# Prompt attention: the gate is scaled by 1/sum before the products, two low-query buffers change places, and three gate writes change queues

## The chip, the cores and the metric

The kernel runs on one core of a Trainium2 chip. The metric is the device time of one execution in microseconds (us). Before the change the median of three runs is 2872.78 us (2870.52 to 2873.95).

The core has five engines with an instruction stream each: TensorE (PE, matrix products and transposes; PEld are its weight loads), VectorE (DVE), ScalarE (ACT), GpSimd (POOL) and SyncE (SP, which here only issues DMAs). An engine runs its instructions in the order of its stream, and an instruction that waits holds up all that stand behind it. PSUM is the memory that PE writes its products to.

## The reference

The kernel is one step of a two-layer decoder over a prompt of 1024 rows (with 16 meta rows ahead of it) and 64 sample rows. Layer one is an mLSTM mixer with a feed-forward block, layer two a "forgetting attention" with a gate, and a feed-forward block again. The change lies in the prompt's attention of layer two:

```python
def fox_attention(q, cq, pos_q, k, v, ck, pos_k):           # cut: one block of 128 query rows
    s = einsum('bqhd,bkhd->bhqk', qi, k)
    s = s + ci[..., None] - ckT[:, :, None, :]
    s = where(pos_k[None, :] <= pi[:, None], s, -inf)
    p = softmax(s, axis=-1)
    return einsum('bhqk,bkhd->bqhd', p, v)

def fox_mixer(xn, shared, attend, w_qo, q_g, w_out):
    ...
    og = p[..., HD:]
    o = attend(q, k, v, lf).reshape(B, T, HD)
    return (o * jax.nn.sigmoid(og)) @ w_out
```

There are 16 heads of 64 columns. The softmax is not normalised before the product with v: the kernel forms exp(s - max) v, and the division by the row's sum is folded into the gate's factor, so that each output element is (exp(s - max) v) * sigmoid(og) * 1/sum. Which of the two factors comes first does not matter to the mathematics.

## The kernel before, in words

**Where the part lies.** `attend_prompt` (L2456) runs from about 1770 to 2023 us of the profiled execution. Ahead of it stands the sample rows' attention, in which PE's gaps are filled with the gate projections `gates()` (L2089): for seven of eight blocks of 128 gate columns, PE multiplies, ACT takes the sigmoid (L2105) and POOL's queue writes it to the tensor `og2D` in device memory (L2106). Behind `attend_prompt` comes the output projection and the last feed-forward block.

**Units.** Heads are taken in pairs (`hp` 0 to 7), and the two heads of a pair are called z = 0 and 1; they lie on partitions 0 to 63 and 64 to 127 of the query and key tiles. Query rows are taken in groups of 256 (`g`, in the order QG = 0, 3, 1, 2), each of two blocks u of 128 rows. A group g has g + 1 units of up to 256 keys; the last unit of a group is its tail. That makes 32 groups, each with a tail, and 80 units.

**Score pieces.** `scores()` cuts a block's keys into pieces of up to 512 (KSPLIT). A piece takes two PSUM buffers named `sp`, one for each z, out of three. PE writes both with six matmuls (L2596: high queries by high keys, high queries by low keys, low queries by high keys). Then DVE, first for z = 0 and then for z = 1, adds the forget terms (`ncb`, or `nd` on the diagonal), keeps the row's maximum (L2600, each with a short read of the maximum into `mx`) and so frees the buffer. POOL computes the exponent's bias `nb` and the next diagonal `nd` (L2566); ACT takes the exponentials and their sums `sm` (L2623).

**A unit.** `turn` transposes the exponentials on PE into a PSUM tile `tp` (L2650, L2654; there are two such tiles, of two banks each); ACT copies it to `th` (L2658), and at a tail 16 further rows to `tail` (L2660). At a tail DVE also takes the reciprocal of the sums (L2663, `r`) and POOL spreads it over 64 columns (L2666, `rx`). `prod` multiplies `th` with the values into the PSUM tile `op` (L2683 to L2691; there is one such tile, shared by all groups, so the next group's first product waits until DVE has read it).

**The tail before the change.** `prod` first transposes `rx` on PE with four small matmuls (L2678): two go into the free part of `tp` (head 0 of the pair), two into the free part of `op` (head 1). After the products DVE computes `og = op * og` on 128x256 (L2694) and then twice `og = rs * og` on 128x128 (L2697), once with rs out of `tp`, once out of `op`. POOL then splits the result into a high and a low part.

**Order.** PE, DVE, ACT and POOL run this part in the order in which the code is written. The loop over groups and units writes, for each unit: score pieces that are due (`ahead`), the unit's `turn`, exponentials, further pieces (`ahead`), and then the `prod` of the unit before (`late`). Pieces run nine ahead (LEAD). Between the first nine pieces stand the steps of `last_gate`, the eighth block of gate columns in 24 steps of three matmuls (L266 to L268): six steps ahead of the first piece and two after each of the nine. Its three sigmoids (L2483) use the `tp` tiles.

**Query and key tiles.** `load_k` loads four tiles of a head pair: high queries, high keys, low keys and, after the forget terms, low queries (`qDl`). Even head pairs use four of the weight slots that earlier phases leave, odd ones four tiles of their own. The last slot, `slots[8]`, is the weight slot that the last gates of `gates()` read.

Of the kernel before, what the change touches and what calls it, by code (L numbers as in the profile page):

```python
# [8 lines left out]
F32R = mybir.dt.float32r  # L9
# [7 lines left out]
P = 128  # L17
# [1946 lines left out]
def phase_b(self, ys, w7, cb):  # L1964
# [121 lines left out]
    with self.pool("spp") as sp, self.pool("sp2", bufs=2) as s2, self.pool("gb", bufs=3) as fp, \  # L2086
            self.pool("spps", bufs=2, space=PSUM) as pp:
        def gates():

            for m in range(7):  # L2090
                if m == 4:

                    self.w7 = gate(7, keep=w7)
                wh, wl = gate(m) if m else w0
                for t, (t0, t1) in enumerate(TS):
                    if (m, t) == (0, 0):
                        continue
                    n = t1 - t0
                    ps = pp.tile([P, 512], F32, name=self.uid("bps"), tag="b", bufs=3)
                    xh, xl = self.X[t]  # L2100
                    for k in range(KT):
                        self.mm3(ps[:, :n], wh[:, k, :], wl[:, k, :], xh[:, k, :], xl[:, k, :], k == 0, k == KT - 1)
                        if k == KT - 1:
                            s = fp.tile([P, SL], F32, name=self.uid("ogb"), tag="ogb")
                            nc.scalar.activation(s[:, :n], ps[:, :n], AF.Sigmoid)  # L2105
                            nc.gpsimd.dma_start(self.og2D[m, :, t0:t1], s[:, :n])  # L2106
                        yield

        with self.tc.manual_schedule(engines={mybir.EngineType.PE}):
            self.attend_sample(sk, sp, s2, pp, cq, ncn, masks, ys, gates())  # L2110
# [345 lines left out]
def attend_prompt(self, ys, slots, both, w):  # L2456
# [3 lines left out]
    with self.pool("ap", bufs=1) as sp, self.pool("ap2", bufs=2) as s2, self.pool("app", bufs=2, space=PSUM) as pp:  # L2460
# [34 lines left out]
        heads = {}  # L2495

        def place_k(hp):
            if hp % 2 == 0:
                return [slots[x][:, :NP] for x in (2, 7, 3, 8)]
            return [s2.tile([P, NP], F32R, name=f"{nm}_{hp}", tag=f"{nm}1", bufs=1) for nm in ("qh", "kh", "kl", "ql")]  # L2500

        def place_c(hp):
            return s2.tile([P, 2, NP], F32, name=f"ncb_{hp}", tag="ncb1", bufs=1) if hp % 2 else both
# [31 lines left out]
        firstv = [s2.tile([P, 9, P], F32, name="vr0", tag="vr")]  # L2535
        firsto = [s2.tile([P, 256], F32, name="og0_0", tag="ogP", bufs=8)]
        first[1], firstc[1] = place_k(1), place_c(1)
        for qb in (6, 5, 7):
            firsts.update({(qb, z): row(0, qb, z) for z in range(2)})
        for qb in (3,):  # L2540
# [26 lines left out]
                                        in1=mask.unsqueeze(1).broadcast_to([P, 2, P]), op=ALU.add)  # L2567

        rows = {}

        def scores(hp, g):

# [6 lines left out]
            for u in range(2):  # L2579
# [11 lines left out]
                for n in KSPLIT[qb]:  # L2591
                    ps = [pp.tile([P, 512], F32, name=f"sp{hp}_{qb}_{c}_{z}", tag="sp", bufs=3) for z in range(2)]
                    for y, (a, b) in enumerate(((qh, kh), (qh, kl), (ql, kh))):
                        for z in range(2):
                            r = slice(z * 64, z * 64 + 64)
                            nc.tensor.matmul(ps[z][:, :n], a[r, qs], b[r, at : at + n], start=(y == 0), stop=(y == 2))  # L2596
                    parts = [(0, n)] if at + n < nk else [(0, n - P), (n - P, n)]
                    for z in range(2):
                        for y, (o, e) in enumerate(parts):
                            nc.vector.tensor_tensor_reduce(  # L2600
                                out=ss[z, u][:, at + o : at + e], in0=ps[z][:, o:e],
                                in1=diag[x][:, z] if y else ncb[:, z, at + o : at + e], scale=1.0,
                                scalar=mx[:, z, c + y - 1 : c + y] if c + y else NEG, op0=ALU.add, op1=ALU.max,
                                accum_out=mx[:, z, c + y : c + y + 1])
# [21 lines left out]
        def units(hp, g):  # L2626
# [8 lines left out]
            for j0 in range(0, nf, 2):  # L2635
# [3 lines left out]
                def turn(j0=j0, tail=tail, hold=hold):  # L2639
# [19 lines left out]
                    if tail:  # L2659
# [5 lines left out]
                            [P, 2, 2, DH], F32, name=f"rx{hp}_{g}", tag="rx")  # L2665
                        nc.gpsimd.tensor_copy(rx, hold["r"].unsqueeze(3).broadcast_to([P, 2, 2, DH]))  # L2666

                def prod(j0=j0, tail=tail, hold=hold):
                    th = hold["th"]
                    mm = nc.tensor.matmul  # L2670
                    if tail:


                        hold["rs"] = [hold["pt"][:, 0, 6:], po[:, 256:384].rearrange("p (u q) -> p u q", u=2)]
                        for u in range(2):
                            for h, x in enumerate(hold["rs"]):
                                r = slice(h * 64, h * 64 + 64)
                                mm(x[:, u], hold["rx"][r, u].rearrange("p z d -> p (z d)"), self.ident[r, r],  # L2678
                                   start=(h == 0 or j0 == 0), stop=True, is_transpose=True, skip_group_check=True)
                    ds = [slice(z * 64, z * 64 + 64) for z in range(2)]  # L2680
                    for x in range(1 if tail else 2):
                        for z in range(2):
# [9 lines left out]
                               start=False, stop=(u == 1))  # L2692
                    y = og[g]
                    nc.vector.tensor_tensor(out=y, in0=po[:, :256], in1=y, op=ALU.mult)  # L2694
                    for h, x in enumerate(hold["rs"]):
                        yh = y.rearrange("p (u h q) -> p h u q", u=2, h=2)[:, h]
                        nc.vector.tensor_tensor(out=yh, in0=x, in1=yh, op=ALU.mult)  # L2697
                    c0 = T0 + 256 * g
                    for t, (t0, t1) in enumerate(TS):
                        a, b = max(c0, t0), min(c0 + 256, t1)  # L2700
# [5 lines left out]
                            nc.gpsimd.tensor_tensor(out=xl[:, hp, xs], in0=ya, in1=xh[:, hp, xs].bitcast(F32),  # L2706
                                                    op=ALU.subtract)

                out.append((turn, prod))
            return out  # L2710

        groups = [(hp, g) for hp in range(8) for g in QG]
# [10 lines left out]
        with tc.manual_schedule(engines={E.PE, E.DVE, E.Activation, E.Pool}):  # L2723
# [4 lines left out]
                masked(x)  # L2728
            todo, gate = pieces(), last_gate()
            made = 0  # L2730
            for _ in range(6):
                next(gate, None)

            def ahead(slot):

                nonlocal made
                while made < ns and made < LEAD + slot * ns / (2 * nu):
                    next(todo, None)
                    made += 1
                    if slot == 0:  # L2740
                        for _ in range(2):
                            next(gate, None)
                        exps(len(todo_exp) - 1)

            late = None
            slot = 0
            todo_exp = []
            for hp, g in groups:
                us = None
                for k in range(g + 1):  # L2750
# [13 lines left out]
                        n = max(n - m, 0)  # L2764
                    us[k][0]()
                    exps(n)
                    ahead(slot + 1)
                    if late:
                        late()
                    late = us[k][1]  # L2770
                    slot += 2
                    if g == QG[1] and k == 2 and hp < 7:
                        load_v(hp + 1, nc.sync)
# [7 lines left out]
            late()  # L2781
    return ws


# [32 lines left out]
```

## Time and profile before

| | before |
|---|---|
| median of three runs | 2872.78 us |
| profiled execution, its own time | 2874.75 us |
| its span in the profile | 2873.1 us |
| mean granted clock of TensorE | 0.997 |
| instructions in the profile | 53648 |
| median of the runs less the profiled execution | -1.97 us |

The span is the stretch from the first to the last instruction of the profiled execution, and 1.65 us of its own time lie around it. A row of the timeline names a start and a duration in us, the engine, the line of the kernel, the operation, the output tile and its inputs, the shape and how many stand in the row; in square brackets stands the idle time of the engine just ahead of it and what ended that idle time. The view of the waits lists, for one engine, the line that waited, the instruction that released it, the sum in us, the number of times and the longest. The view by stretches gives the busy time of PE, PEld, DVE, ACT and POOL in a stretch, each with its number of instructions, and then the granted clock, the share of busy DMA engines and GB/s. The ends of PE's instructions are modelled, and neighbours overlap in the rows, so that starts are read rather than ends.

### The profile page before, as it was taken

How to read it: one execution, taken by the hardware profiler on the slowest of the kernel's cores; microseconds unless marked ns; L12 is line 12 of the kernel's file. 1: busy time of each engine (PE TensorE's matmuls, PEld its weight loads, DVE VectorE, ACT ScalarE, POOL GpSimd, SP SyncE). 2: the span in 40 equal slices, each digit the busy share in tenths (PEclk: the TensorE clock that was granted, in tenths of full speed). 3: DMA queues.
4: the chain of work that ended last, by engine and by line, in shares of the span. 5: the costliest groups of instructions: out<-in, count | busy, mean ns of one | idle time of the engine just before them, and what ended most of it. 6: DMA issues, size and time to landing. Idle time of an engine off the chain costs nothing.

```text
span 2873.1 us, 53648 instructions
## 1 busy us (share of the span) xinstructions
PE 2795.3 (97%) x20485; PEld 2674.7 (93%) x20485; DVE 1726.0 (60%) x3478; ACT 1310.9 (46%) x2622; POOL 1017.8 (35%) x1495
## 2 busy tenths in 40 slices
PE   7999989999999999999999999999999999999999
PEld 7998979999999999999999888677999999999999
DVE  6044555887777655553345444776478777765553
ACT  6122464444444434443444444777344444443432
POOL 3022333075556311115352102454307655531210
PEclk9999999999999999999999999999999999999999
DMA  7057656122222275544453676442413222237652
GB/s 214 16 144 170 164 159 182 49 88 78 79 84 78 98 264 197 203 150 136 139 174 123 238 279 220 143 148 85 158 48 94 75 75 84 78 98 255 219 184 101
DMA packets 312443, 400.19 MB, mean 139 GB/s; under 512 B 28142, under 2 KB 235050, under 8 KB 311162
## 3 DMA queue, kind: packets, MB, share of 16 engines
q1 hardware_dynamic: 277234, 277.79, 30.4%
q0 software_dynamic: 33728, 118.38, 12.6%
q8 instruction: 161, 2.64, 0.4%
q14 instruction: 96, 0.79, 0.1%
q10 hardware_dynamic: 1224, 0.60, 0.1%
HBM read 299.92 MB, written 96.77 MB: 138 GB/s over the span
## 4 chain that ended last, share of the span: by engine, by line
PE 69%; DVE 10%; issue 4%; ACT 3%; DMA 2%; POOL 1%; DVEq 0%; ACTq 0%; POOLq 0%; SPq 0%
PE m L1505 23%; PE dps L266 6%; PE dps L268 6%; PE dps L267 6%; PE tmps L266 3%; PE tmps L267 3%; PE tmps L268 3%; DVE slot L339 2%; PE sp L2596 1%; DVE s L2600 1%; PE op L2683 1%; PE pops L266 1%; PE pops L267 1%; PE pops L268 1%; PE bps L266 1%
## 5 line engine op out<-in xcount | busy, mean ns | idle before, releaser
L339 DVE TENSOR_TENSOR slot<-slot,slot 128x1024 fp32r<-128x1024 f32 (+3 forms) x263 | 266.5, 1016 | 133.9 <-ACT slot L338 125.4
L338 ACT CAST slot<-slot 128x1024 fp32r<-128x1024 f32 (+3 forms) x263 | 206.7, 788 | 236.3 <-PE dps L267 90.1
L1505 PE MATMUL m<-x1h,slot 128*128 128x384 f32 x640 | 178.3, 338 | 3.1 <-DVE ns L1481 1.5
L1505 PE MATMUL m<-x0h,slot 128*128 128x336 f32 x640 | 167.0, 316 | 0.0
L413 POOL TENSOR_TENSOR ns<-ns,nq 128x384 f32<-128x384 f32 (+1 forms) x59 | 63.8, 1081 | 210.9 <-ACT nq L411 209.7
L1505 PE MATMUL m<-x2h,slot 128*128 128x384 f32 x480 | 135.8, 337 | 0.0
L1612 POOL DMA_DIRECT2D hr<-hT x60 | 32.5, 542 | 281.6 <-DVE T_2l L339 68.8
L108 POOL TENSOR_TENSOR slot<-vA 128x256 f32<-128x256 f32 x80 | 74.9, 946 | 151.2 <-DMA vA<-in_w_gate_up 147.5
L108 POOL TENSOR_TENSOR slot<-Ht 128x256 f32<-128x256 f32 x80 | 74.9, 946 | 150.9 <-DMA Ht<-in_w_gate_up 147.2
L339 DVE TENSOR_TENSOR slot<-Ht,slot 128x256 fp32r<-128x256 f32 (+3 forms) x101 | 84.9, 842 | 63.6 <-ACT slot L338 63.6
L339 DVE TENSOR_TENSOR slot<-vA,slot 128x256 fp32r<-128x256 f32 (+3 forms) x101 | 85.5, 849 | 62.2 <-ACT slot L338 62.2
L1505 PEld LDWEIGHTS m<-x1h,slot 128*128 128x128 f32 x640 | 117.1, 188 | 4.4 <-DVE ns L1481 2.1
L1505 PEld LDWEIGHTS m<-x0h,slot 128*128 128x128 f32 x640 | 113.3, 188 | 0.0
L1505 PE MATMUL m<-x1l,slot 128*128 128x384 f32 x320 | 107.8, 337 | 0.0
L1505 PE MATMUL m<-x0l,slot 128*128 128x336 f32 x320 | 101.0, 316 | 0.0
L1505 PE MATMUL m<-T_2h,slot 128*128 128x384 f32 x320 | 96.8, 343 | 3.0 <-ACT Ht L1511 0.9
L2623 ACT ACTIVATE s<-s,nb 128x272 f32<-128x272 f32 (+7 forms) x126 | 98.9, 786 | 0.1
L2658 ACT COPY th<-tp 128x768 f32<-128x768 f32 (+1 forms) x80 | 73.4, 919 | 55.3 <-PE tp L2650 32.6
L1505 PE MATMUL m<-T_4h,slot 128*128 128x384 f32 x320 | 95.3, 338 | 0.0
L108 POOL TENSOR_TENSOR Ht<-Ht 128x512 f32<-128x512 f32 (+1 forms) x60 | 84.5, 1408 | 28.4 <-DVE wl1l L339 28.4
L108 POOL TENSOR_TENSOR vA<-vA 128x512 f32<-128x512 f32 (+1 forms) x60 | 84.4, 1408 | 27.5 <-DVE wl0l L339 27.5
L2029 DVE TENSOR_REDUCE ss<-sqb 128x4 f32<-128x256 f32 (+1 forms) x72 | 30.2, 419 | 102.8 <-ACT sqb L2028 102.0
(843 smaller groups left out, 10286.8 us busy)
## 6 DMA issues: line engine op xcount, KB each, us to landing
slot<-in_w_down SPq DMA_DIRECT2D x88, 512.0 KB, 4.4
wr<-in_w_down SPq DMA_DIRECT2D x42, 512.0 KB, 4.7
wraw<-in_w_in_a SPq DMA_DIRECT2D x40, 512.0 KB, 4.0
vA<-in_w_gate_up SPq DMA_DIRECT2D x40, 512.0 KB, 3.9
Ht<-in_w_gate_up SPq DMA_DIRECT2D x40, 512.0 KB, 4.1
hr<-hT POOLq DMA_DIRECT2D x46, 384.0 KB, 5.5
kp<-in_cache_k SPq DMA_DIRECT2D x32, 512.0 KB, 5.6
vp<-in_cache_v SPq DMA_DIRECT2D x32, 512.0 KB, 6.3
```

The source lines that it names most:

```text
L108: self.net.nc.gpsimd.tensor_tensor(out=o, in0=a, in1=b, op=op)
L266: mm(ps, sh, mh, start=first, stop=False)
L267: mm(ps, sh, ml, start=False, stop=False)
L268: mm(ps, sl, mh, start=False, stop=last)
L338: self.nc.scalar.copy(hi, src)
L339: self.nc.vector.tensor_tensor(out=lo, in0=src, in1=hi.bitcast(F32), op=ALU.subtract)
L413: (nc.vector if x >= late else nc.gpsimd).tensor_tensor(out=s, in0=s, in1=sq, op=ALU.add)
L1505: nc.tensor.matmul(u.b[b][:, :n], w[p][:, k], x[q][:, k], start=new and k == i == 0, stop=k == 1 and i == 2, skip_group_check=True)
L1612: nc.gpsimd.dma_start(hraw[j], hT[t][:, 2 * c : 2 * c + 2])
L2029: nc.vector.tensor_reduce(out=ss[:m, i, :], in_=sq[:m].rearrange("p (h d) -> p h d", d=DH), op=ALU.add, axis=AX.X)
L2623: nc.scalar.activation(ss[z, u], ss[z, u], AF.Exp, bias=nb[:, z : z + 1], accum_out=sm[:, u, z : z + 1])
L2658: nc.scalar.copy(th.rearrange("p x z (u h q) -> p h (x z u) q", h=2, q=64)[:, :, :n], pt[:, :, :n])
```

## The change

1. **The tail.** The four transposes of `rx` (now `spread`) all go into the free part of `tp`, which has room for both heads. They are written into PE's stream right after the six matmuls of the first score piece that follows the tail's `turn`. The two multiplications of the gate by 1/sum (now `scale`) are written into DVE's stream between that piece's z = 0 and z = 1 (or, where no piece follows, ahead of the products, `flush`). After the products there is one multiplication on DVE, `og = op * og`. So `op` is read by one DVE instruction and `tp` by two that come before the products' result.
2. **Low queries.** The fourth tile of even head pairs is a tile of their own and that of odd ones is `slots[8]`. The tiles of head pair 0 are set aside early, so its low queries no longer land in the slot that the last gates read.
3. **Gate steps.** Three, not six, steps of `last_gate` stand ahead of the first score piece; the three left over follow the ninth piece.
4. **Queue.** The three writes of the seventh gate block (m = 6) are issued by ACT instead of POOL.

```diff
-                            nc.gpsimd.dma_start(self.og2D[m, :, t0:t1], s[:, :n])
+                            (nc.scalar if m == 6 else nc.gpsimd).dma_start(self.og2D[m, :, t0:t1], s[:, :n])
...
         def place_k(hp):
+            own = lambda nm: s2.tile([P, NP], F32R, name=f"{nm}_{hp}", tag=f"{nm}1", bufs=1)
             if hp % 2 == 0:
-                return [slots[x][:, :NP] for x in (2, 7, 3, 8)]
-            return [s2.tile([P, NP], F32R, name=f"{nm}_{hp}", tag=f"{nm}1", bufs=1) for nm in ("qh", "kh", "kl", "ql")]
+                return [slots[x][:, :NP] for x in (2, 7, 3)] + [own("ql")]
+            return [own(nm) for nm in ("qh", "kh", "kl")] + [slots[8][:, :NP]]
...
+        first[0] = place_k(0)
...
                     parts = [(0, n)] if at + n < nk else [(0, n - P), (n - P, n)]
+                    spread, scale = between.pop() if between else (None, None)
+                    if spread:
+                        spread()
                     for z in range(2):
+                        if z and scale:
+                            scale()
                         for y, (o, e) in enumerate(parts):
...
+                def spread(j0=j0, hold=hold):
+                    hold["rs"] = [hold["pt"][:, h, 6:] for h in range(2)]
+                    for u in range(2):
+                        for h, x in enumerate(hold["rs"]):
+                            r = slice(h * 64, h * 64 + 64)
+                            nc.tensor.matmul(x[:, u], hold["rx"][r, u].rearrange("p z d -> p (z d)"), self.ident[r, r],
+                                             start=True, stop=True, is_transpose=True, skip_group_check=True)
+
+                def scale(hold=hold):
+                    for h, x in enumerate(hold["rs"]):
+                        yh = og[g].rearrange("p (u h q) -> p h u q", u=2, h=2)[:, h]
+                        nc.vector.tensor_tensor(out=yh, in0=x, in1=yh, op=ALU.mult)
+
                 def prod(j0=j0, tail=tail, hold=hold):
                     th = hold["th"]
                     mm = nc.tensor.matmul
-                    if tail:
-
-
-                        hold["rs"] = [hold["pt"][:, 0, 6:], po[:, 256:384].rearrange("p (u q) -> p u q", u=2)]
-                        for u in range(2):
-                            for h, x in enumerate(hold["rs"]):
-                                r = slice(h * 64, h * 64 + 64)
-                                mm(x[:, u], hold["rx"][r, u].rearrange("p z d -> p (z d)"), self.ident[r, r],
-                                   start=(h == 0 or j0 == 0), stop=True, is_transpose=True, skip_group_check=True)
...
                     y = og[g]
                     nc.vector.tensor_tensor(out=y, in0=po[:, :256], in1=y, op=ALU.mult)
-                    for h, x in enumerate(hold["rs"]):
-                        yh = y.rearrange("p (u h q) -> p h u q", u=2, h=2)[:, h]
-                        nc.vector.tensor_tensor(out=yh, in0=x, in1=yh, op=ALU.mult)
...
-            for _ in range(6):
+            for _ in range(3):
                 next(gate, None)
...
+            def flush():
+                for pair in between:
+                    for f in pair:
+                        f()
+                between.clear()
...
+                    if late and late[2]:
+                        between.append(late[2])
                     ahead(slot + 1)
                     if late:
-                        late()
-                    late = us[k][1]
+                        flush()
+                        late[1]()
+                    late = us[k]
```

VectorE's stream at the tail of group 3 of head pair 0. `og_3` is the gate's tile, `op_3` the products, `tp_3_6` the tail's transposes, `sp_7_0_0` and `sp_7_0_1` the first piece of query block 7 for z = 0 and 1, `sp_7_1_0` its second piece. Before:

```order
L2600 ISA s_7_0_19140,mx_7_19142<-sp_7_0_0_19143,ncb_18561 128x512
L2600 ISA mx_7_19142 128x1
L2600 ISA s_7_1_19141,mx_7_19142<-sp_7_0_1_19144,ncb_18561 128x512
L2600 ISA mx_7_19142 128x1
L2694 TENSOR_TENSOR og_3_18595<-op_3_18893,og_3_18595 128x256
L2697 TENSOR_TENSOR og_3_18595<-tp_3_6_19058,og_3_18595 128x2x64
L2697 TENSOR_TENSOR og_3_18595<-op_3_18893,og_3_18595 128x2x64
L2600 ISA s_7_0_19140,mx_7_19142<-sp_7_1_0_19170,ncb_18561,mx_7_19142 128x272
```

The same place after the change:

```order
L2608 ISA s_7_0_19141,mx_7_19143<-sp_7_0_0_19144,ncb_18560 128x512
L2608 ISA mx_7_19143 128x1
L2687 TENSOR_TENSOR og_3_18595<-tp_3_6_19058,og_3_18595 128x2x64 x2
L2608 ISA s_7_1_19142,mx_7_19143<-sp_7_0_1_19145,ncb_18560 128x512
L2608 ISA mx_7_19143 128x1
L2706 TENSOR_TENSOR og_3_18595<-op_3_18893,og_3_18595 128x256
L2608 ISA s_7_0_19141,mx_7_19143<-sp_7_1_0_19171,ncb_18560,mx_7_19143 128x272
```

Two multiplications went from behind the products' multiplication to ahead of the z = 1 half of the piece; there are as many as before.

ScalarE's stream at the start of the prompt's attention. `ogb` are the last gates of the seventh block, `th` and `og7s` the sigmoids of the eighth, `s_1` and `s_2` the first exponentials. Before:

```order
L2105 ACTIVATE ogb_18475<-bps_18398 128x384
L2105 ACTIVATE ogb_18518<-bps_18478 128x384
L2483 ACTIVATE th_18575<-og_18606 128x336
L2623 ACT_TABLE_LOAD
L2623 ACTIVATE s_1_0_18576,smf<-s_1_0_18576,nbf 128x144
L2623 ACTIVATE s_1_1_18577,smf<-s_1_1_18577,nbf 128x144
L2623 ACTIVATE s_2_0_18578,smf<-s_2_0_18578,nb_2_18662 128x272
L2623 ACTIVATE s_2_1_18579,smf<-s_2_1_18579,nb_2_18662 128x272
L2483 ACT_TABLE_LOAD
L2483 ACTIVATE og7s_18753<-og_18667 128x384
```

After:

```order
L2105 ACTIVATE ogb_18475<-bps_18398 128x384
L2106 DMA og2D<-ogb_18475 128x384
L2105 ACTIVATE ogb_18518<-bps_18478 128x384
L2106 DMA og2D<-ogb_18518 128x384
L2631 ACT_TABLE_LOAD
L2631 ACTIVATE s_1_0_18576,smf<-s_1_0_18576,nbf 128x144
L2631 ACTIVATE s_1_1_18577,smf<-s_1_1_18577,nbf 128x144
L2483 ACT_TABLE_LOAD
L2483 ACTIVATE th_18575<-og_18606 128x336
L2631 ACT_TABLE_LOAD
L2631 ACTIVATE s_2_0_18578,smf<-s_2_0_18578,nb_2_18653 128x272
L2631 ACTIVATE s_2_1_18579,smf<-s_2_1_18579,nb_2_18653 128x272
```

The first exponentials went ahead of the eighth block's first sigmoid, which costs two more table loads, and the writes of the seventh block came into this stream.

More of the change, by code (lines that the diff above doesn't have):

```diff
@@ L2569, in attend_prompt @@
         rows = {}
+        between = []
         def scores(hp, g):
@@ L2707, in prod @@
                                                     op=ALU.subtract)
-                out.append((turn, prod))
+                out.append((turn, prod, (spread, scale) if tail else None))
             return out
@@ L2780, in attend_prompt @@
                     next(tile0)
-            late()
+            for f in late[2]:
+                f()
+            late[1]()
     return ws
```

## The prediction

> **What bounds the kernel.** I read the page's first part, then the view by stretches, then the waits of TensorE inside the prompt's attention, then the timelines of the places that these name.
>
> ```profile
> span 2873.1 us, 53648 instructions
> PE 2795.3 (97%) x20485; PEld 2674.7 (93%) x20485; DVE 1726.0 (60%) x3478; ACT 1310.9 (46%) x2622; POOL 1017.8 (35%) x1495
> 1870.00:1910.00 40.00, 37.52 (x524) 27.85 (x521) 29.72 (x147) 28.81 (x59) 20.46 (x54) 1.00 0.41 138
> 2030.00:2070.00 40.00, 40.00 (x246) 39.81 (x245) 20.24 (x29) 13.22 (x20) 13.69 (x18) 1.00 0.54 180
> ```
>
> PE sets the time: 97% busy in all, 37.52 of 40 us inside the attention, 40.00 of 40 behind it. The change removes no product, so it can win only what PE idles in the attention, and what it wins there stays won, since the stretch behind is full of PE's own work. The waits there (1765 to 2030 us):
>
> ```profile
> PE sp L2596 <- DVE mx L2600: 7.2, 17, 0.9
> PE tp L2650 <- DVE og L2697: 4.0, 7, 0.6
> ...
> PE op L2683 <- PE sp L2596: 1.0, 6, 0.2
> PE sp L2596 <- DMA slot<-qDl: 0.6, 1, 0.6
> ...
> PE op L2683 <- DVE r L2663: 0.5, 1, 0.5
> ...
> PE op L2683 <- DVE og L2697: 0.4, 2, 0.2
> ```
>
> These rows hold 13.7 us, an upper end for any gain. The sum is made against the profiled execution, 2874.75 us by its own time, which is 1.97 us above the median of the runs (2872.78).
>
> **DVE at a tail.** The first rows are DVE's, the last five POOL's, ACT's and PE's, at one group-3 tail:
>
> ```profile
> 1867.78 0.69 DVE L2600 CUSTOM_DVE_ANT_0 s<-sp,ncb 128x512 f32<-128x512 f32 x1 [1.07 <-PE op L2678]
> 1868.39 0.69 DVE L2600 CUSTOM_DVE_ANT_0 s<-sp,ncb 128x512 f32<-128x512 f32 x1
> 1869.01 0.42 DVE L2694 TENSOR_TENSOR og<-op,og 128x256 f32<-128x256 f32 x1
> 1869.53 0.29 DVE L2697 TENSOR_TENSOR og<-tp,og 128x128 f32<-128x128 f32 x1
> 1869.74 0.28 DVE L2697 TENSOR_TENSOR og<-op,og 128x128 f32<-128x128 f32 x1
> 1869.94 0.49 DVE L2600 CUSTOM_DVE_ANT_0 s<-sp,ncb,mx 128x272 f32<-128x272 f32 x1
> 1865.80 0.40 POOL L2666 COPY rx<-r 128x256 f32<-128x256 f32 x1
> 1865.15 0.25 ACT L2660 COPY tail<-tp 16x128 f32<-16x128 f32 x1
> 1867.47 0.21 PE L2678 MATMUL tp<-ident,rx 64*128 64x64 f32 x1
> 1870.14 0.44 PE L2596 MATMUL sp<-kh,qh 64*128 64x384 f32 x1
> 1871.09 0.41 PE L2596 MATMUL sp<-kh,qh 64*128 64x384 f32 x1 [0.50 <-DVE mx L2600]
> ```
>
> The first 128x128 multiplication starts 0.10 us after the end of the 128x256 one (1869.53 against 1869.01 + 0.42), whose result it needs. Where an instruction needs nothing of the one ahead, it starts 0.08 us before that one's end (1868.39 against 1867.78 + 0.69; 1869.74 against 1869.53 + 0.29). After the change the 128x128 pair needs only `rx`, and the 128x256 one needs only the second of the pair, behind which a whole score reduction lies. So each tail costs DVE 0.52 - 0.34 = 0.18 us less (I count 0.17): 0.21 + 0.20 + 0.34 in place of the 0.93 from 1869.01 to 1869.94. The ends are 0, if an instruction always waits for the one ahead, and 0.18, since the same three multiplications stay.
>
> The Trainium skill, "VectorE: DVE Perf Modes", section "The DRAIN you can't avoid", says that the pipe is flushed after every DVE instruction whatever the semaphores, so that only fewer instructions help; by it this term would be 0. The trace disagrees at these rows: 0.10 us behind the end in one case, 0.08 ahead of it in the other.
>
> **What of it reaches PE.** Three places.
>
> At this one (the second half of the piece that follows, which waits for a `sp` buffer that DVE reduces behind the tail) the 0.50 wait shrinks by 0.17. It stands at the group-3 tails of pairs 0 to 6: 7 x 0.17 = 1.2 us. Ends: 0 and 7 x 0.18 = 1.3.
>
> The next two places lie behind a group-2 tail and behind the group-0 tail after it:
>
> ```profile
> 1884.94 0.56 DVE L2600 CUSTOM_DVE_ANT_0 s<-sp,ncb 128x400 f32<-128x400 f32 x1
> 1885.43 0.57 DVE L2600 CUSTOM_DVE_ANT_0 s<-sp,ncb 128x400 f32<-128x400 f32 x1
> 1884.97 0.71 PE L2650 MATMUL tp<-ident,s 64*128 64x64 f32 x16 [0.57 <-DVE og L2697]
> 1885.46 0.49 PE L2596 MATMUL sp<-kh,qh 64*128 64x256 f32 x2
> ...
> 1888.30 0.28 DVE L2697 TENSOR_TENSOR og<-op,og 128x128 f32<-128x128 f32 x1
> 1888.73 1.08 PE L2683 MATMUL op<-th,vr 128*64 128x256 f32 x8 [0.16 <-PE sp L2596]
> ```
>
> Behind group 2, the turn waits 0.57 us until the gate's multiplication has read `tp` (the 4.0 us, 7 times). That read moves ahead, so this wait goes. But the score piece right behind the turn starts at 1885.46, as soon as DVE's reduction of 1884.94 has given its buffer back (the next one starts at 1885.43), and this reduction comes only 0.17 us earlier. I take 7 x 0.17 = 1.2 us; the other 0.4 of each should reappear as a wait of L2596 for `mx`. Ends: 0 and 7 x 0.57 = 4.0, if the piece finds a buffer free. The value is near the low end, since the reduction's row and the piece's start nearly touch.
>
> Behind group 0, group 3's first product waits 0.16 us for `op` (1.0 + 0.4 us, 8 times, put down to various releasers). The tile now comes free when the 128x256 multiplication ends, 0.17 us sooner. That is the whole wait: 8 x 0.17 = 1.4 us. Ends: 0 and 1.4.
>
> **What the moved work could cost.** The pair now holds up the z = 1 reduction by 0.21 + 0.21 = 0.42 us at every tail. In the rows above, its buffer came free at 1868.39 + 0.69 = 1869.08 and would at 1869.50, while PE asks for it at 1870.14: covered by 0.64. I cost it at nothing; with the cover gone, it is 0.42 at each tail (a rival below). The moved transposes at 1867.47 need `rx`, ready at 1865.80 + 0.40 = 1866.20, and now also that the 16 rows were copied out of `tp` (1865.15 + 0.25): 1.3 and 2.1 us of room. POOL's split of the result waits for the 128x256 multiplication alone, 0.2 us sooner.
>
> **The start.** PE, ACT and POOL as the attention begins, and an ACT-issued DMA from another phase for its price:
>
> ```profile
> 1773.77 0.54 POOL L2106 DMA_DIRECT2D og2D<-ogb  x1 [4.76 <-issue]
> 1774.50 0.34 PE L2596 MATMUL sp<-slot,slot 64*128 64x144 f32 x2 [0.65 <-DMA slot<-qDl]
> 1776.06 0.45 ACT L2483 ACTIVATE th<-og 128x336 f32<-128x336 f32 x1 [4.78 <-PE og L268]
> 1783.95 1.28 ACT L2483 ACT_TABLE_LOAD   x1 [4.00 <-issue]
> 1792.84 0.49 ACT L2483 ACTIVATE og7s<-og 128x384 f32<-128x384 f32 x1
> 1794.45 0.68 PE L2650 MATMUL tp<-ident,s 64*128 64x64 f32 x14
> 1.43 0.34 ACTq L291 DMA_DIRECT2D grows<-in_norm_ffn  x1
> ```
>
> The 0.65 wait for the low queries goes, because their tile is free early and nothing else there is late: the same piece's other four matmuls did not wait. What is late next is ACT's third sigmoid of the eighth block, whose `tp` the turn at 1794.45 takes over. The second sigmoid's gate steps end later by two pieces of some 0.8 us and sooner by 0.65, so ACT's chain from 1783.95 on moves some 0.9 back, and the third ends near 1793.33 + 0.5 = 1793.8, which is when the turn is now wanted (1794.45 - 0.65). I take 0.5 of the 0.65. Ends: 0.65 and, with the chain another 0.9 late, a loss of 0.3.
>
> Two more table loads of 1.28 lie in ACT's gaps of 4.78 and 4.00: nothing. ACT issues three DMAs at 0.34 each, two of them in the 4.78 gap and the first in the sample rows' stage: nothing, for each stands right behind its own sigmoid, and what is queued behind are the table load and the first exponentials, which have no scores yet. POOL loses 3 x 0.54 and a wait ahead of the diagonals: nothing on PE's path. The SP queue keeps its number of DMAs. The eighth block's write on POOL slips behind two small bias operations: its first reader is the last head pair's gates.
>
> **The end.** The last tails have no score piece behind them:
>
> ```profile
> 2017.05 0.43 DVE L2694 TENSOR_TENSOR og<-op,og 128x256 f32<-128x256 f32 x1 [0.25 <-PE op L2691]
> 2017.71 0.28 DVE L2697 TENSOR_TENSOR og<-op,og 128x128 f32<-128x128 f32 x1
> 2018.14 1.08 PE L2683 MATMUL op<-th,vr 128*64 128x256 f32 x8 [0.50 <-DVE r L2663]
> ```
>
> `op` is free at 2017.99 before and near 2017.56 after, once the pair fits ahead with little wait: 0.4 us of the 0.50. Ends: 0 and 0.5.
>
> **Sum.** 1.2 + 1.2 + 1.4 + 0.5 + 0.4 = 4.7 us. The profiled execution goes from 2874.75 to 2870.05, the median to 2872.78 - 4.7 = 2868.1 us, 0.16% less. About 0.2% (5.7 us; 2867.0 and 2878.5) is what a measurement of this kernel tells from no change. My own range for this case is 2866.3 to 2869.6 (gains of 3.2 to 6.5): the low gain has the start at -0.3 and half of the 1.4 missing, the high one has the wait behind group 2 shrink by 0.4 instead of 0.17 and the start at its 0.65.
>
> **Rivals.** *The waits vanish whole.* If the pieces behind group 2 find their buffer, 4.0 + 1.4 + 1.2 + 0.65 + 0.5 = 7.8 us go: 2865.0. For it speaks that the 0.57 is charged to `og` alone; against it the reduction's start beside the piece's. Also POOL's bias work follows DVE's maxima, and could move with them.
>
> *DVE saves nothing at a tail* (the flush rule above). Then only the start and the end remain, 0.9 us: 2871.9, and the waits for `og` turn into waits for `mx`. The 0.10 and 0.08 of the rows speak against it.
>
> *The pair blocks a score buffer* (slower). DVE holds the z = 1 half 0.42 us longer at all 32 tails. If PE wanted that buffer more than 0.64 us sooner than at the place shown, each tail would lose it: 32 x 0.42 - 0.9 = 12.5 us, 2885.3. At places where several short pieces stand behind a tail I know the room less well, and PE that gains elsewhere asks sooner. Half of the tails give 2878.6, the point from which it is slower.
>
> *The change does nothing*: the low queries' DMA has its early tile but waits for something else, and ACT's sigmoids cost the turn what was won. It lies inside the second rival's time, and shares its chance.
>
> **Chances.** Forecast 0.50, vanishing waits 0.25, no saving 0.13, blocked buffer 0.12. Of the forecast's own range about a quarter lies below 2867.0 (0.12) and counts as faster: faster 0.25 + 0.12 = 0.37; same 0.38 + 0.13 = 0.51; slower 0.12. The range 2864.0 to 2872.5 takes in the first three cases and leaves out the fourth and the tails of the others.
>
> **What would show it.** DVE's gap of 0.10 before L2687 gone, and 0.76 for the three multiplications together; no wait of the turn (L2658) for `og`; L2599 waiting 0.3 to 0.4 for `mx` at 1885; group 3's first product without a wait; no wait for `qDl`. Wrong I would be if L2599's waits for `mx` grow beyond 7.2 + 2.8 us, or if a wait for `rx` or the third sigmoid appears on PE.

## The result, and the profile after

The changed kernel takes 2864.39 us (median of 20 runs, 2860.56 to 2871.11), the kernel before 2869.39 us (20 runs, 2865.48 to 2873.95). The ratio is 0.9985 with a 95% interval of 0.9979 to 0.9992: 4.3 us less, between 2.3 and 6.0. The forecast was 4.7 us less, a ratio of 0.9984. (The three runs known beforehand, median 2872.78, lay high among the 20; hence the ratio, not the absolute time, is compared.)

The first part of the page of the kernel after:

```profile
span 2864.7 us, 53623 instructions
PE 2798.8 (98%) x20485; PEld 2679.3 (94%) x20485; DVE 1724.8 (60%) x3478; ACT 1313.7 (46%) x2624; POOL 1014.7 (35%) x1492
```

The view of TensorE's waits in the prompt's attention (1760 to 2025 us), after:

```profile
PE sp L2599 <- DVE mx L2608: 7.6, 23, 0.9
PE tp L2681 <- POOL rxf L2674: 1.2, 1, 1.2
PE tp L2681 <- POOL rx L2674: 1.1, 1, 1.1
PE op L2695 <- ACT th L2666: 0.2, 1, 0.2
PE tp L2681 <- ACT tail L2668: 0.2, 1, 0.2
```

Gone are the turns' waits for `og`, the first products' waits for `op` (1.0 and 0.4 us before), a turn's wait of 1.1 us for `th` near the end, the end's wait for `r` and the wait for the low queries. The wait for `mx` comes 23 times instead of 17, which is the wait that was to reappear behind group 2, and two waits for POOL's copy of 1/sum are new or longer: 1.2 us at the start, 1.1 (before 0.4) at the end.

VectorE at the group-3 tail whose rows the prediction quotes, and PE behind it, after:

```profile
1863.83 0.69 DVE L2608 CUSTOM_DVE_ANT_0 s<-sp,ncb 128x512 f32<-128x512 f32 x1 [1.05 <-PE tp L2681]
...
1864.45 0.48 DVE L2687 TENSOR_TENSOR og<-tp,og 128x128 f32<-128x128 f32 x2
1864.85 0.68 DVE L2608 CUSTOM_DVE_ANT_0 s<-sp,ncb 128x512 f32<-128x512 f32 x1
...
1865.45 0.42 DVE L2706 TENSOR_TENSOR og<-op,og 128x256 f32<-128x256 f32 x1
1865.79 0.49 DVE L2608 CUSTOM_DVE_ANT_0 s<-sp,ncb,mx 128x272 f32<-128x272 f32 x1
...
1866.94 0.41 PE L2599 MATMUL sp<-kh,qh 64*128 64x384 f32 x1 [0.32 <-DVE mx L2608]
```

The pair takes 0.40 us (1864.45 to 1864.85) and the 128x256 multiplication 0.34 (1865.45 to 1865.79): 0.74 in place of 0.93. PE's wait is 0.32 in place of 0.50.

PE behind the group-2 tail, and at the first products behind the tails of groups 1 and 0, after:

```profile
1871.48 0.66 PE L2658 MATMUL tp<-ident,s 64*128 64x64 f32 x16
1872.07 1.08 PE L2695 MATMUL op<-th,vr 128*64 128x256 f32 x8
...
1879.89 0.65 PE L2658 MATMUL tp<-ident,s 64*128 64x64 f32 x16
1880.35 0.36 PE L2599 MATMUL sp<-kh,qh 64*128 64x256 f32 x1
1881.02 0.38 PE L2599 MATMUL sp<-kh,qh 64*128 64x256 f32 x1 [0.31 <-DVE mx L2608]
...
1883.93 1.08 PE L2695 MATMUL op<-th,vr 128*64 128x256 f32 x8
```

The turn behind group 2 no longer waits, and the piece behind it waits 0.31 us in its second half. The same places before, for the first product behind group 1:

```profile
1875.62 0.66 PE L2650 MATMUL tp<-ident,s 64*128 64x64 f32 x16
1876.42 1.08 PE L2683 MATMUL op<-th,vr 128*64 128x256 f32 x8
```

From turn to product it is 0.80 us before and 0.59 after, although no view put a wait there: PE's ends are modelled and covered the idle 0.21 us.

How long the attention takes is read between two starts that both kernels share, the last sample product (L2440) and the first product of the output projection (L266). Before, then after:

```profile
1768.90 1.07 PE L2440 MATMUL pom<-ptM,vmS 16*128 16x32 f32 x8
2022.53 0.43 PE L266 MATMUL pops<-x0h,slot 128*128 128x336 f32 x1
```

```profile
1766.00 1.07 PE L2440 MATMUL pom<-ptM,vmS 16*128 16x32 f32 x8
2013.38 0.42 PE L266 MATMUL pops<-x0h,slot 128*128 128x336 f32 x1
```

That is 253.63 and 247.38 us. Cut at the first score piece of each head pair (the first row of a 64x144 `sp`), the parts are:

| stretch | before | after | difference |
|---|---|---|---|
| last sample product to the scores of pair 1 | 33.50 | 35.78 | +2.28 |
| scores of pair 1 to pair 2 | 29.06 | 28.05 | -1.01 |
| pair 2 to pair 3 | 31.62 | 29.31 | -2.31 |
| pair 3 to pair 7 (four periods) | 115.54 | 112.13 | -3.41, 0.85 each |
| pair 7 to the output projection | 43.91 | 42.11 | -1.80 |
| sum | 253.63 | 247.38 | -6.25 |

So the tails win 0.85 us in every period, and the start loses. These are single executions: the 31.62 of the third row holds a stretch of low clock that the kernel after has elsewhere (below). The 2.9 us by which the two kernels differ ahead of the attention can't be put to the change: two executions of one and the same kernel (tail and places, below) get there at 1770.06 and 1766.10 us.

### The profile page after: what moved, and what is told of

Its sections match the earlier page's. It is cut to its first block, busy times and chain, and to the rows that moved or that the text cites. A ratio compares the mean times of both kernels' runs of the same rounds, so it can differ in the third digit from the quotient of the medians.

```text
span 2864.7 us, 53623 instructions
## 1 busy us (share of the span) xinstructions
PE 2798.8 (98%) x20485; PEld 2679.3 (94%) x20485; DVE 1724.8 (60%) x3478; ACT 1313.7 (46%) x2624; POOL 1014.7 (35%) x1492
## 4 chain that ended last, share of the span: by engine, by line
PE 71%; DVE 9%; issue 4%; ACT 4%; DMA 2%; POOL 1%; DVEq 0%; ACTq 0%; POOLq 0%; SPq 0%
PE m L1505 24%; PE dps L266 6%; PE dps L268 6%; PE dps L267 6%; PE tmps L266 3%; PE tmps L267 3%; PE tmps L268 3%; PE sp L2599 2%; PE op L2695 2%; DVE slot L339 1%; PE pops L266 1%; PE pops L267 1%; PE pops L268 1%; PE bps L266 1%; PE tp L2658 1%
```

## The experiments

Theory 1 is the prediction's: the tail's work on DVE is 0.18 us shorter and frees `op` and `tp` sooner. It was widened after the profile by the place behind group 1 and by the start's new wait. The table gives for each run the ratio to the kernel before in runs on the same chip, with its 95% interval, and, from one profile each, the length of the attention as above and a period: the middle one of the four from pair 3 to pair 7. (In five of the profiles one of the four is longer, by 0.33 to 0.36.)

| run | ratio | attention, us | a period |
|---|---|---|---|
| changed kernel | 0.9985 (0.9979 to 0.9992) | 247.38 | 28.03 |
| tail alone | 0.9977 (0.9968 to 0.9986) | 246.78 | 28.04 |
| start alone | 1.0013 (1.0004 to 1.0022) | 253.31 | 28.88 |
| pair behind z = 1 | 0.9993 (0.9984 to 1.0002) | 250.71 | 28.63 |
| both halves in `tp` only | 0.9988 (0.9979 to 0.9997) | 248.88 | 28.53 |
| eighth block's writes on ACT too | 0.9978 (0.9968 to 0.9988) | 247.36 | 28.03 |
| seventh block's writes on POOL | 0.9980 (0.9971 to 0.9989) | 248.64 | 28.03 |
| tail and places | 0.9970 (0.9957 to 0.9982) | 245.23 | 28.02 |
| tail and places, again | 0.9978 (0.9969 to 0.9987) | 246.69 | 28.02 |
| tail and queue | 0.9982 (0.9973 to 0.9991) | 245.30 | 28.03 |
| six gate steps | 0.9976 (0.9966 to 0.9986) | 244.22 | 28.04 |
| changed kernel, again | 0.9981 (0.9971 to 0.9990) | 247.53 | 28.02 |

**The tail alone.** The other three parts are undone:

```diff
-(nc.scalar if m == 6 else nc.gpsimd).dma_start(self.og2D[m, :, t0:t1], s[:, :n])
+nc.gpsimd.dma_start(self.og2D[m, :, t0:t1], s[:, :n])
...
-                return [slots[x][:, :NP] for x in (2, 7, 3)] + [own("ql")]
-            return [own(nm) for nm in ("qh", "kh", "kl")] + [slots[8][:, :NP]]
+                return [slots[x][:, :NP] for x in (2, 7, 3, 8)]
+            return [own(nm) for nm in ("qh", "kh", "kl", "ql")]
...
-        first[0] = place_k(0)
...
-            for _ in range(3):
+            for _ in range(6):
                 next(gate, None)
```

> Only the tail is changed (transposes of rx and the pair of multiplications early, both halves in tp); queues, low-query places and the six gate steps are as before. Theory 1 (the tail's DVE chain is 0.18 us shorter and op comes free after one multiplication): the four places of a head pair shrink as in the changed kernel, a period of 28.0 us against 28.9, that is 0.85 x 7 to 8 = 6 to 7 us less than before (ratio 0.9977), with the 0.65 us wait for the low queries still there and no wait of PE for rxf at the start. Rival (the gain needs the whole change, or comes from the start): ratio 0.9990 or more.

Ratio 0.9977, 6.6 us less (4.0 to 9.2); the period is 28.04, the wait for the low queries is there (0.51 us), and none for `rxf`. Theory 1 holds, and the whole gain is the tail's.

**The start alone.** The kernel before with the other three parts (the same diff, the other way round).

> Only the start is changed (low-query places, three gate steps, the seventh gate block's writes on ACT's queue); the tail is as before. Theory 1: the 0.65 us wait for the low queries goes, and a wait of some 1.2 us of PE for rxf comes, because POOL's 393rd DMA, which takes 2.5 us longer to start, is now the last write of the eighth gate block and stands ahead of rxf: 0.3 to 0.6 us slower than before, ratio 1.0000 to 1.0004, period 28.9. Rival (the start wins and the tail loses): 0.9980 to 0.9990, no wait for rxf.

Ratio 1.0013, 3.7 us more (1.1 to 6.3): slower, by more than the 0.3 to 0.6 expected. The wait is where it was expected, and POOL's rows of this run show its cause:

```profile
1794.56 0.57 POOL L2484 DMA_DIRECT2D og2D<-og7s  x1 [6.24 <-issue]
1795.13 0.41 POOL L2668 COPY rxf<-rf 128x256 f32<-128x256 f32 x1
```

```profile
1791.59 0.49 ACT L2483 ACTIVATE og7s<-og 128x384 f32<-128x384 f32 x1
```

The sigmoid ended at 1792.08 and the write that needs it started at 1794.56, 2.48 us later; elsewhere such a write follows its sigmoid by some 0.3 us (before: 1792.84 + 0.49 to 1793.63). `rxf` stands behind the write on POOL, and PE behind `rxf`. In the kernel before, the same delay is at 1773.77, 2.49 us behind the sigmoid of 1770.79 + 0.49. Counted along POOL's instructions, both are the 393rd DMA that POOL issues. Of the 3.7 us, the profile shows 0.54 at the first product (27.71 us after the last sample product, 27.17 before) and 1.23 at the first scores of pair 1 (34.73, 33.50 before), a part of it by the clock (below). The rest stands in no view: the attention as a whole is here 0.3 us shorter than before, whose profile holds the low clock in its 31.62.

**The pair behind z = 1.** As the changed kernel, but:

```diff
                     for z in range(2):
-                        if z and scale:
-                            scale()
                         for y, (o, e) in enumerate(parts):
...
+                    if scale:
+                        scale()
                     at += n
```

> As the changed kernel, but on DVE the pair of multiplications by 1/sum stands behind both halves of the score piece, next to the multiplication that needs its result. Theory 1 (the gain is the 0.18 us that a dependent neighbour costs): the 0.10 us gap comes back, the period goes back to 28.6 to 28.9, and the time is that of before, ratio 0.9995 to 1.0005. Rival A (it is enough that the pair comes before the products): period 28.0, ratio 0.9985. Rival B (holding up the z = 1 half costs 0.4 us a tail): faster than the changed kernel, ratio below 0.9975.

Ratio 0.9993 and a period of 28.63. DVE at a group-3 tail of this run:

```profile
1858.27 0.48 DVE L2687 TENSOR_TENSOR og<-tp,og 128x128 f32<-128x128 f32 x2
1858.86 0.42 DVE L2706 TENSOR_TENSOR og<-op,og 128x256 f32<-128x256 f32 x1
1859.20 0.49 DVE L2606 CUSTOM_DVE_ANT_0 s<-sp,ncb,mx 128x272 f32<-128x272 f32 x1
```

The 128x256 multiplication starts 0.11 us after the pair's end (1858.75), the three together take 0.93 again (1858.27 to 1859.20), and PE's wait there is back at 0.51. Both rivals fall: it is not enough that the pair comes ahead, and holding up the z = 1 half costs less than the gap does. Behind group 2 the turn waits only 0.24 for `tp` in place of 0.57, but nothing of that is won: from the products ahead of that turn to those behind it the starts lie 3.67 us apart, as before (3.46 in the changed kernel). The 0.25 us a period that stays is read from the first products behind groups 1 and 0, which start 0.17 and 0.10 us sooner than before. Why these stay was not tested.

**Both halves in `tp`, nothing else.** The kernel before with:

```diff
-                        hold["rs"] = [hold["pt"][:, 0, 6:], po[:, 256:384].rearrange("p (u q) -> p u q", u=2)]
+                        hold["rs"] = [hold["pt"][:, h, 6:] for h in range(2)]
...
-                                   start=(h == 0 or j0 == 0), stop=True, is_transpose=True, skip_group_check=True)
+                                   start=True, stop=True, is_transpose=True, skip_group_check=True)
```

> As before, but both halves of the transposed rx go into tp; the pair still stands behind the 128x256 multiplication. Theory 1: op comes free after one multiplication, so the first products behind the tails of groups 1 and 0 start 0.2 us sooner each (period 0.45 us shorter), while the turn behind group 2 waits 0.2 us longer for tp, since the second of the pair now reads it too: net period 28.6 to 28.7, 1.5 to 2.5 us less than before, ratio 0.9992. Rival (op is not what those products wait for): period 28.9 to 29.1, ratio 1.0000 or more.

Ratio 0.9988, a period of 28.53. The turn behind group 2 waits longer, as expected, and no product waits for `op`:

```profile
PE sp L2596 <- DVE mx L2600: 7.2, 17, 0.9
PE tp L2650 <- DVE og L2697: 5.4, 7, 0.8
```

So the tile that the first products wait for is `op`. By the starts, they come 0.20 us sooner behind group 1 and 0.24 behind group 0, as in the changed kernel, and the products behind group 2's turn 0.10 later (3.77 in place of 3.67): 0.44 won and 0.10 lost a period.

**The eighth block's writes on ACT too.** As the changed kernel, but:

```diff
-                nc.gpsimd.dma_start(self.og2D[7, :, t0:t1], s[:, :n])
+                nc.scalar.dma_start(self.og2D[7, :, t0:t1], s[:, :n])
```

> As the changed kernel, and the three writes of the eighth gate block are issued by ACT's queue too, so POOL's 393rd DMA comes long after the first tail. Theory 1 (that DMA's 2.5 us stand ahead of rxf): PE's 1.2 us wait for rxf goes, the first product starts 27.85 - 1.4 = 26.4 us after the last sample product instead of 27.85, and the time is 1.2 to 3 us below the changed kernel's, ratio to before 0.9974 to 0.9981. Rival (rxf is late for another reason, the reciprocal or the sums): the wait stays, ratio 0.9985.

The wait for `rxf` goes, as theory 1 has it, but the first product comes 27.74 us after the last sample product, not 26.4. PE waits directly ahead instead:

```profile
1786.72 0.71 PE L2658 MATMUL tp<-ident,s 64*128 64x64 f32 x16 [0.90 <-ACT og7s L2483]
```

That is the third sigmoid. The 393rd DMA of POOL is in this run a write behind the attention (`hD`, L569, at 2023.38 us), and 5.12 us marked "issue" stand ahead of it: the delay has moved on with the count. The attention is as long as in the changed kernel (247.36), while the ratio is 0.9978 with an interval that overlaps; whether this version is faster stays open.

**The seventh block's writes on POOL.** As the changed kernel, with only its first line of the diff undone.

> As the changed kernel, but the three writes of the seventh gate block are issued by POOL, as before. Theory 1: the slow 393rd DMA is again the third of these, some 5 us after the last sample product; the wait for rxf goes, but POOL makes the first diagonals 2 us later than in the changed kernel while the first scores come 1.4 us earlier than before, so PE waits about 1 us for a score buffer at the second or third piece: within 0.5 us of the changed kernel, ratio 0.9983 to 0.9988. Rival (the third gate write does not hold up the scores): 1.2 us better, 0.9980.

The slow DMA is back at the third of these writes (4.76 us idle ahead of it, as before), POOL makes the first diagonals late, and PE waits 1.72 us at the second piece; for `rxf` 0.16. The wait was 0.7 longer than expected, and yet the ratio, 0.9980, is not worse than the changed kernel's. Its interval does not tell the two apart.

**The tail and the places**, with POOL's writes and six gate steps as before.

> The tail and the low-query places are changed; queue and the six gate steps are as before. Theory 1: as the tail alone, less the 0.5 us wait for the low queries, with the slow DMA where it was before: ratio 0.9973 to 0.9977, the best of all so far. Rival (the places by themselves cost, since low queries now land among other transfers): 0.9980 or more.

Ratio 0.9970. The 0.51 wait for the low queries goes; 0.34 of it comes back as a wait for the first maxima, because POOL's slow DMA still stands ahead of the first diagonal.

**The tail and the queue**, with the places and the six gate steps as before.

> The tail and the queue of the seventh gate block's writes are changed; places and the six gate steps are as before. Theory 1: the slow DMA moves to the last write of the eighth block, PE waits 1 to 2 us for rxf behind the fourteenth piece: 1 to 3 us slower than the tail alone, ratio 0.9981 to 0.9988. Rival (it is the three gate steps that make rxf late): as the tail alone, 0.9977, no wait for rxf.

Ratio 0.9982. The slow DMA is the eighth block's last write, as expected, but PE waits 0.34 us for `rxf`, not 1 to 2: with six steps ahead, the sigmoids come earlier relative to the turn. The wait needs the queue and the three steps together. The low queries cost 0.90.

**The clock.** Start alone loses more than its waits; the granted clock is the next thing to read. PE's two long waits at the start and the view by stretches (the clock is the third value from the end), of the kernel after, then the stretch of start alone:

```profile
1790.18 0.60 PE L2599 MATMUL sp<-slot,slot 64*128 64x400 f32 x3 [0.86 <-DVE mx L2608]
1793.44 0.47 PE L2681 MATMUL tp<-ident,rxf 64*128 64x64 f32 x4 [1.23 <-POOL rxf L2674]
```

```profile
1790.00:1795.00 5.00, 3.48 (x39) 2.64 (x41) 3.41 (x19) 4.19 (x7) 2.01 (x5) 0.74 0.12 43
1795.00:1800.00 5.00, 5.00 (x46) 3.55 (x44) 1.67 (x7) 4.30 (x11) 2.21 (x5) 0.57 0.10 28
```

```profile
1795.00:1800.00 5.00, 4.41 (x46) 3.58 (x48) 1.87 (x10) 4.89 (x11) 2.88 (x9) 0.66 0.13 44
```

At the 0.86 us wait for `mx` and the 1.23 us wait for `rxf`, which follow each other within 4 us, the clock goes down to half: (1 - 0.74) x 5 + (1 - 0.57) x 5 = 3.45 us of full clock lost in the kernel after, 1.7 in start alone. At half clock these are stretches of 6.9 and 3.4 us. In the kernel after, the clock falls before the second wait is over: it is 0.50 from 1792.5 on, and the wait ends at 1793.44. The time lost is less than the clock lost: from the first product to the scores of pair 1 the kernel after takes 7.93 us and six gate steps (below), with the full clock, 5.77, so 2.16 less. In the kernel before, this place has 1.00, and its low stretch in the attention lies later, at two waits of 0.69 and 0.60:

```profile
1840.00:1845.00 5.00, 4.40 (x36) 2.78 (x37) 2.30 (x13) 1.02 (x3) 2.21 (x6) 0.66 0.30 107
```

Two such waits stand at that place in all thirteen profiles (0.67 to 0.69, then 0.47 to 0.67), and the low clock comes with them in three: before, tail alone, and the second run of tail and places. So these shorter waits do not settle it.

The Trainium skill, "TensorE: Matmul & The Clock Gate", Part 1 on the HAM clock gate, says that PE falls to half clock after an idle window of about 3.4 us. The lengths of the stretches here, 3.4 and 6.9 us, agree with such a window; that it has to be idle does not, since no PE wait at this place is longer than 1.23 us.

That two long waits close upon each other bring the half clock is theory 2; the last three runs test it.

**The changed kernel again.**

> The changed kernel once more. Theory 2 (the 0.86 and 1.23 us waits in a row at the start bring PE's granted clock down to 0.5 for 3.4 us or twice that): the low clock stands at the same place, directly behind the wait for rxf, and the time is again 0.9980 to 0.9990 of before. Rival (the low clock is chance, a property of single executions): no low clock between 1780 and 1800 us, or at another place.

Ratio 0.9981, and the low clock stands at the same place:

```profile
1790.00:1795.00 5.00, 2.87 (x42) 2.20 (x37) 3.15 (x16) 4.19 (x6) 0.97 (x3) 0.95 0.08 21
1795.00:1800.00 5.00, 4.93 (x46) 3.72 (x48) 1.86 (x8) 4.72 (x11) 3.25 (x9) 0.50 0.13 44
1800.00:1805.00 5.00, 5.00 (x65) 3.31 (x61) 2.94 (x18) 2.25 (x6) 0.85 (x4) 0.87 0.49 161
```

**The tail and the places again.**

> The kernel with the tail and the places changed, once more, on the chip of the changed kernel. Theory 2: PE's longest wait at the start is 0.9 us and stands alone, the clock stays at 1.00 from 1780 to 1800, and the time is 1 to 4 us below the changed kernel's (ratio 0.9970 to 0.9978). Rival (the start makes no difference): the same ratio as the changed kernel's.

Ratio 0.9978. No low clock from 1780 to 1800, but one at 1835 to 1845, at the place where the kernel before has it; in the first run of this kernel there was none in the attention. Against the changed kernel on the same chip that is 1.7 us less by the medians (2863.96 against 2865.61), within the intervals.

**Six gate steps.** As the changed kernel, with `range(6)` in place of `range(3)`.

> The changed kernel with six steps of the eighth gate block ahead of the first score piece in place of three. Theory 2: the slow 393rd DMA is ready for 1 us sooner relative to PE, PE waits 0.2 to 0.5 us for rxf in place of 1.23, the clock stays at 1.00 there, and the time is 2 to 4 us below the changed kernel's (0.9972 to 0.9978). Rival (three steps are what gains at the start): as the changed kernel or slower, 0.9985 or more.

Ratio 0.9976, the median 3.3 us below the changed kernel's on the same chip (2862.34 against 2865.61), the intervals overlapping. The wait for `rxf` is 0.35 us, the clock stays up, and its attention is the shortest of all:

```profile
1763.44 1.07 PE L2440 MATMUL pom<-ptM,vmS 16*128 16x32 f32 x8
2007.66 0.43 PE L266 MATMUL pops<-x0h,slot 128*128 128x336 f32 x1
```

```profile
1785.00:1790.00 5.00, 3.68 (x57) 2.87 (x56) 2.79 (x14) 3.30 (x6) 1.21 (x4) 1.00 0.15 40
```

All profiles in which PE waits 0.9 us or more once again right behind the 0.86 us wait show the half clock at this place (changed kernel twice, start alone, pair behind z = 1, eighth block on ACT); those without it do not (before, tail alone, both halves in `tp`, tail and places twice, tail and queue, six steps; the seventh block on POOL has its half clock behind the 1.72 wait). That is a pattern over thirteen profiles of eleven kernels; the rule that makes it was not isolated, and elsewhere in the kernel half clock comes and goes between executions: of the two of tail and places, one has it at 1645 us and not at 605, the other at 605 and not at 1645.

## Why the prediction came out as it did

**The total** was right: 4.7 us less forecast, 4.3 (2.3 to 6.0) measured, within 0.2%. It was right as a sum of two terms that were both off: the tail won more (6.6 alone, 4.0 to 9.2, forecast 4.2 with the end; by the profile 0.85 us in each period, where the sum has 3 x 0.17 = 0.51) and the start lost 3.7 alone, where a gain of 0.5 was forecast. That the two errors nearly cancel is luck. One of the prediction's own signs of being wrong did appear: a wait for `rx` on PE, 1.23 us at the start.

**DVE at a tail**: right. 0.93 became 0.74, and the run with the pair behind z = 1 shows that it is the gap ahead of the dependent neighbour. The second rival falls by that run, and with it the flush rule as the prediction took it from the Trainium skill: the same number of instructions, 0.19 us apart.

**Behind group 3**: 0.50 became 0.32, forecast 0.33. **Behind group 2**: the wait for `tp` went and 0.31 us came back as a wait for `mx`, forecast 0.4; by the starts of what follows, 0.21 us is won, forecast 0.17. The first rival (whole waits vanish) falls here. **Behind group 0**: 0.24 by the starts, forecast 0.16 to 0.17.

**What was missed in the tails**: the first product behind group 1 also waited for `op`, 0.21 us in each of seven pairs, 1.5 us in all (in pair 7 it is the 0.50 wait of the end). The step that failed is the list of three places: it was taken from the view of waits, where modelled ends hid this one. For the same reason the 13.7 us were no upper end for any gain; besides, the rows that the prediction left out hold another 2.2 us.

**The moved work**: right. Holding up z = 1 by 0.4 us cost nothing at the places seen, and the third rival (the pair blocks a score buffer) falls. So does the fourth, that the change does nothing: the wait for the low queries went.

**The start**: wrong in sign. "The 0.65 wait for the low queries goes" held, and the first turn comes 0.89 us earlier. "What is late next is ACT's third sigmoid" named the wrong engine: it was POOL, through a write whose start is 2.5 us late and which the moved queue had put ahead of `rxf`. The step "POOL loses 3 x 0.54 and a wait ahead of the diagonals: nothing on PE's path" is the one that failed; that wait (the 4.76 us marked "issue") was not removed but moved. The third sigmoid is next in line, 0.90 us, once POOL is out of the way. And the half clock at the waits, 1.7 to 3.45 us of clock, had no term in the sum.

**The end**: 1.80 us less from the first scores of pair 7 on, a stretch that holds tails of pairs 6 and 7 too, so the 0.4 of the sum can't be read apart. The 0.50 wait went, and the wait for `rx` grew from 0.45 to 1.09, since the reciprocal stands behind a weight split on DVE. The sum also left out a turn that before waits 1.07 us for `th`:

```profile
2012.63 0.59 PE L2650 MATMUL tp<-ident,s 64*128 64x64 f32 x12 [1.07 <-ACT th L2658]
```

It stays in start alone and with both halves in `tp` only, and is gone in every kernel that scales the gate ahead of the products. Why it hangs on that stays open.

## What to carry to other kernels

Price a moved instruction also by what its neighbours on the new engine and the old one do next: a wait marked "issue" that no releaser explains may belong to the queue's count, and moves on to another instruction when DMAs are taken off the queue. Two multiplications that depend on each other are cheaper with something independent between them, and a tile that the next group needs is best read by one instruction. Measure gains between starts of instructions, since modelled ends hide waits of 0.2 us, and look at the granted clock behind every new wait on TensorE.

## What the runs showed of the hardware that I had not expected

The 393rd DMA that POOL issues starts 2.48 to 2.49 us later than the end of the sigmoid that it waits for, whichever transfer it is: the seventh block's last write in the kernels that leave this block to POOL, the eighth block's last write in the others. With both blocks on ACT it is a later write, with 5.12 us marked "issue" ahead of it. Why was not found; only that it goes by the count. Half the clock was granted for one or two stretches of about 3.4 us at waits of 0.86 and 0.90 to 1.23 us that followed each other within 4 us (five profiles of five) and behind a single one of 1.72 us; at waits of 0.67 to 0.69 and 0.47 to 0.67 us it came in three profiles of thirteen.
